# A hybrid layer on one core: the output projection's squares, norms and first feed-forward weights are rearranged, and the last attention chains change their queue

## The chip, the cores and the metric

The kernel runs on one core of one Trainium2 chip. The metric is the device time of one execution in microseconds (us), less is better. The core has TensorE (PE; its weight loads are listed as PEld), VectorE (DVE), ScalarE (ACT), GpSimd (POOL) and SyncE (SP). In this kernel SP issues nearly every DMA, in one order that is fixed when the program is built.

## The reference

One layer over 2,048 frames with 16 learned meta tokens in front (T = 2,064), width 1,024, in float32. What matters here is cut from it:

```python
p = rms_norm(h, norm_mix_pre) @ w_in                     # oa: RG-LRU, ob: attention, oc: RWKV-7, from slices of p
mixed = jnp.concatenate([oa, ob, oc], axis=-1) @ w_out   # the output projection
h = h + rms_norm(mixed, norm_mix_post)
f = causal_dwconv(rms_norm(h, norm_ffn_pre) @ ffn_up, ffn_conv)    # 2 x 2816 columns, 3 taps
gate, val = jnp.split(f, 2, axis=-1)
f = (jax.nn.gelu(gate, approximate=True) * val) @ ffn_down
h = h + rms_norm(f, norm_ffn_post)
```

Here `rms_norm(x, g) = x * rsqrt(mean(x * x) + 1e-6) * g`. The attention group has 8 heads of width 64, is causal, and its softmax is weighted by forget gates.

## The kernel before

Every large product is made of three float32r products: an operand is split into a high part (a copy by ACT, L1594 or L166) and a low part (the difference, by DVE or POOL, L1595 or L167), and `mm3` multiplies high by high (L172), high by low (L173) and low by high (L174). The program is written out in full in Python, and each engine's list of instructions is put in its final order when the program is built: a scheduler that works with estimated durations takes, for each engine, the instruction that comes first in the source among those that it holds ready. On the chip each engine then goes through its own list strictly in order, and waits at an instruction whose inputs are not there, whatever stands ready behind it. `tc.issue_after(ins)` keeps instructions behind `ins` in the list of its engine.

The stages that the change touches, in order of time:

- **End of the attention** (class `Attn`). For each head and each block of 512 queries, `weights` makes scores (L681, L682), exponentials on ACT (L686), the products with v (`po`, L704) and, on POOL and partly DVE, the sum of the exponentials (`acc`, L725). When a block's last group is through, `ending` puts three steps on a list that is worked off later: `total` (the sum over partitions by PE, L751 and L752, then the DMAs `scr_den<-acc`, L754, and `dcol<-scr_den`, L755), `invert` (reciprocal, then the DMAs L760 and L761) and `scale` (multiply, then the DMA L765 into `scr_mix`). Each of the five DMAs needs the one before it to have landed. `ending` of one block runs inside `weights` of the next block, after its first group of scores. The last two blocks of all are those of head 7: queries 1,040 to 1,551 and 1,552 to 2,063.
- **Output projection** (`w_out_tile`): 17 tiles of tokens in `FFN_TILES`, the first with 2 rows, the others with 128. A tile loads its slice of `scr_mix` (L165, one buffer `raw`), splits it into `mh` and `ml` (two buffers each), multiplies by the resident weights `woh`, `wol` (48 matmuls of 512 columns into two banks `pswo`), then `add_normed` squares both banks (ACT, L1513, with a sum), scales them (DVE, L1522), adds the residual `wx` (L1523), and `rstd_of` squares the result for the next norm (ACT, L116 or L118). ACT's squares have to be written somewhere: they go into `mh`. Tiles 0 to 6 fill gaps of PE during the attention; tiles 7 and 8 (`HELD`) stay behind the products of the last but one block; tiles 9 to 12 need that block's result, tiles 13 to 16 that of the last block.
- **Norms for the feed-forward** (`ffn_norm`): load a tile of `h` (`xt<-scr_h`, L1555, three buffers), scale it (DVE, L1556), transpose it (PE, L1561), copy it into the quarters `q`. For the first third of the tokens (7 tiles) one such norm follows each output tile from tile 8 (`LATE`) on; after the seventh, `ffn_sums` makes the combined quarters t1 to t4 on POOL (L1589).
- **Feed-forward, up** (`ffn_up`): 3 thirds of the tokens times 22 column blocks of 128 give 66 units. A unit makes four products of quarters by 7 (a Strassen-like scheme, `PRODUCTS`), each of 12 matmuls of 344 columns, in three banks. ACT copies the banks of p1, p5 and p6 into `ga`, `vb` and `u2` before another product is added to them. The weights of the next unit are loaded and split while a unit runs (`ahead.operand`). The 7 weights `ws` and 7 token operands `xs` of the very first unit are made ahead of it. Of their buffers, 4 of 10 for weights (`uw`) and 3 of 8 for tokens (`xo`) exist beside the output projection; the rest takes over its memory. For the second and third part of the tokens, `between` runs one norm at the start of each unit.

Of the kernel before, what the change touches and what calls it, by code (L numbers as in the profile page):

```python
# [18 lines left out]
P = 128  # L19
# [419 lines left out]
class Attn:  # L439
# [209 lines left out]
    def weights(self, h, b, keys, queries, fill):  # L649
# [80 lines left out]
        def ending(po, acc):  # L730
# [13 lines left out]
            rb = []  # L744

            def total():
# [7 lines left out]
                nc.sync.dma_start(scr["den"][h : h + 1, ts], acc[0:1, :n])  # L754
                nc.sync.dma_start(dcol[:, :g], scr["den"][h, ts].rearrange("(p c) -> p c", c=g))  # L755

            def invert():
                rb.append(self.t([64, 512], "rb"))
                nc.vector.reciprocal(dcol[:, :g], dcol[:, :g])
                nc.sync.dma_start(scr["rden"][h, ts].rearrange("(p c) -> p c", c=g), dcol[:, :g])  # L760
                nc.sync.dma_start(rb[0][:, :n], scr["rden"][h : h + 1, ts].broadcast_to([64, n]))  # L761

            def scale():
                nc.vector.tensor_tensor(o[:, :n], o[:, :n], rb[0][:, :n], op=ALU.mult)
                nc.sync.dma_start(scr["mix"][256 + 64 * h : 256 + 64 * h + 64, ts], o[:, :n])  # L765
# [36 lines left out]
    def run(self, pool):  # L802


        ready = []
# [17 lines left out]
        for step in ready:  # L823
            self.weights(*step, lambda share: None)
# [659 lines left out]
def w_out_tile(core, pool, psum, scr, w, x, meta, gain, s, rows, v):  # L1484
# [65 lines left out]
def ffn_norm(core, pool, psum, scr, s, rows, rs, gain, quarters, sup):  # L1550

    nc = core.nc
    xt = pool.tile([P, D], F32, tag="nt_x", name=core.n("xt"))
    t0 = s + META - HALO
    nc.sync.dma_start(xt[:rows], scr["h"][t0 : t0 + rows, :])  # L1555
# [140 lines left out]

POOLED = (3, 6), (6,)
# [10 lines left out]
def ffn_up(core, raws, ring, pool, banks, w_up, cw, scr, between, tokens):  # L1708
# [8 lines left out]
    ws = [ahead.operand(i) for i in range(7)]  # L1717
    xs = [tokens(0, i) for i in range(7)]
# [15 lines left out]
    for at, (sup, j) in enumerate(units):  # L1734
# [9 lines left out]
        for i, (name, (_, _, at_)) in enumerate(PRODUCTS.items()):  # L1744
# [7 lines left out]
            if j == NFF - 1 and more:  # L1752
                xs[i] = tokens(sup + 1, i)
            if more:
                ws_next.append(ahead.operand(i))
            if name == "p1":
                ga = s("ga")
                nc.scalar.activation(ga, ps, AF.Copy)
            elif name == "p5":
                vb = s("vb")  # L1760
                nc.scalar.activation(vb, ps, AF.Copy)
            elif name == "p6":
                u2 = s("u2")
                nc.scalar.activation(u2, ps, AF.Copy)
# [151 lines left out]
LATE = 8  # L1916
# [297 lines left out]
```

## Time and profile before

| | us |
|---|---|
| median of 3 timed runs | 3066.63 |
| lowest, highest | 3063.35, 3073.84 |
| profiled execution, its own time as the page gives it: the span from first to last instruction | 3071.8 |
| PE, DVE, ACT, POOL busy | 2921.6, 2054.8, 1482.3, 1358.8 |
| mean granted TensorE clock | 0.969 |

No time of the profiled execution outside its span is recorded. In the lists of the profile, L172 is line 172 of the kernel before; a bracket such as [6.86 <-ACT xo L1594] gives the time for which the engine stood idle just before the instruction and what ended it. SPq marks DMAs that SP issues; those are not counted as busy.

### The profile page before, as it was taken

The page shows a single profiled execution, that of the slowest core. Times are in us where ns is not written, and L with a number is a line of the kernel's source. Part 1 is how long each engine was busy: PE and PEld are TensorE (multiplying, and loading weights), DVE is VectorE, ACT ScalarE, POOL GpSimd, SP SyncE. Part 2 cuts the span into 40 slices and gives each one's busy share as a digit, 9 for nine tenths or more (in the row PEclk, how much of TensorE's full clock was granted, in tenths as well). Part 3 has the DMA queues.
Part 4 walks back from the last instruction along what each step waited for, and adds up shares of the span by engine and source line. Part 5 has one row for each costly group of instructions (what it writes and reads, how often), then busy time and mean ns, then how long its engine had stood idle before and what let it go on. Part 6 is the DMA issues. An engine that isn't in the chain of part 4 may idle for free. (4 is left out here: it accounts for less than half of the span.)

```text
span 3071.8 us, 52793 instructions
## 1 busy us (share of the span) xinstructions
PE 2921.6 (95%) x18694; PEld 2495.2 (81%) x18694; DVE 2054.8 (67%) x3934; ACT 1482.3 (48%) x2853; POOL 1358.8 (44%) x1589
## 2 busy tenths in 40 slices
PE   6999999999989999999989899999999999999998
PEld 6998898888876654665558899999999998787876
DVE  5268645656667785556635788888778786547766
ACT  4245332443336553555534656666566665324333
POOL 1001121122114555667842457445655444547765
PEclk9998999999988898999999999999999999999999
DMA  6776578466654346535245555566777765435444
GB/s 211 244 237 207 161 244 287 156 211 204 196 153 94 88 104 199 133 99 122 62 129 173 168 182 180 169 201 208 214 215 216 219 189 171 161 104 171 149 160 144
DMA packets 467818, 532.58 MB, mean 173 GB/s; under 512 B 85488, under 2 KB 355514, under 8 KB 466000
## 3 DMA queue, kind: packets, MB, share of 16 engines
q1 hardware_dynamic: 467168, 528.81, 56.5%
q8 instruction: 147, 2.41, 0.3%
q14 instruction: 119, 0.97, 0.1%
q0 software_dynamic: 384, 0.39, 0.0%
HBM read 369.11 MB, written 159.95 MB: 172 GB/s over the span
## 5 line engine op out<-in xcount | busy, mean ns | idle before, releaser
L172 PE MATMUL psu<-xo,uw 128*128 128x344 f32 x1848 | 589.9, 323 | 16.7 <-ACT xo L1594 6.9
L173 PE MATMUL psu<-xo,uw 128*128 128x344 f32 x1848 | 592.6, 321 | 0.0
L174 PE MATMUL psu<-xo,uw 128*128 128x344 f32 x1848 | 582.9, 320 | 0.0
L172 PE MATMUL psp<-xh,wh 128*128 128x384 f32 (+2 forms) x1152 | 383.6, 333 | 4.1 <-ACT wh L166 2.4
L174 PE MATMUL psp<-xh,wl 128*128 128x384 f32 (+2 forms) x1152 | 380.7, 331 | 3.5 <-DMA wl<-scr_wk 3.5
L173 PE MATMUL psp<-xl,wh 128*128 128x384 f32 (+2 forms) x1152 | 380.5, 330 | 0.0
L172 PEld LDWEIGHTS psu<-xo,uw 128*128 128x128 f32 x1848 | 346.9, 188 | 20.3 <-ACT xo L1594 7.1
L1595 DVE TENSOR_TENSOR uw<-uq,uw 128x512 fp32r<-128x512 f32 x341 | 316.2, 933 | 70.3 <-ACT uw L1594 63.7
L173 PEld LDWEIGHTS psu<-xo,uw 128*128 128x128 f32 x1848 | 347.9, 188 | 0.3 <-DVE xo L1595 0.3
L174 PEld LDWEIGHTS psu<-xo,uw 128*128 128x128 f32 x1848 | 346.5, 188 | 0.0
L1594 ACT ACTIVATE uw<-uq 128x512 fp32r<-128x512 f32 x462 | 287.9, 627 | 110.1 <-PE psu L174 48.7
L686 ACT ACTIVATE p<-sc,bias 128x512 f32<-128x512 f32 (+4 forms) x352 | 195.8, 590 | 178.5 <-PE sc L682 146.3
L1725 DVE SCALAR_TENSOR_TENSOR uy<-psu,ffn_cols,uy 128x342 f32<-128x342 f32 (+1 forms) x396 | 223.9, 567 | 60.7 <-ACT uy L1723 59.1
L559 DVE TENSOR_REDUCE mc<-mx 128x1 f32<-128x512 f32 (+6 forms) x352 | 190.3, 565 | 100.9 <-PE mx L554 75.8
L1731 POOL TENSOR_TENSOR uy<-uy,uy 128x342 f32<-128x342 f32 (+1 forms) x132 | 140.6, 1065 | 253.2 <-DVE uy L1725 77.4
L725 POOL TENSOR_TENSOR acc<-acc,p 128x512 f32<-128x512 f32 (+3 forms) x208 | 221.8, 1068 | 60.3 <-ACT p L686 23.9
L1595 POOL TENSOR_TENSOR uw<-uq,uw 128x512 fp32r<-128x512 f32 x121 | 177.9, 1470 | 125.0 <-ACT uw L1594 92.7
L174 PEld LDWEIGHTS psp<-xh,wl 128*128 128x128 f32 x1152 | 222.1, 193 | 13.0 <-issue 6.1
L172 PEld LDWEIGHTS psp<-xh,wh 128*128 128x128 f32 x1152 | 222.1, 193 | 10.7 <-issue 4.0
L173 PEld LDWEIGHTS psp<-xl,wh 128*128 128x128 f32 x1152 | 222.1, 193 | 7.6 <-issue 5.5
L1595 DVE TENSOR_TENSOR fo<-u,fo 128x896 fp32r<-128x896 f32 x88 | 112.6, 1279 | 121.3 <-ACT fo L1594 121.3
L1594 ACT ACTIVATE fo<-u 128x896 fp32r<-128x896 f32 x88 | 81.1, 922 | 206.3 <-POOL u L1841 106.8
(465 smaller groups left out, 6470.4 us busy)
## 6 DMA issues: line engine op xcount, KB each, us to landing
uq<-scr_us SPq DMA_DIRECT2D x220, 256.0 KB
uq<-in_ffn_up_dram SPq DMA_DIRECT2D x209, 256.0 KB
wl<-scr_wk SPq DMA_DIRECT2D x48, 512.0 KB
wh<-scr_wk SPq DMA_DIRECT2D x48, 512.0 KB
u<-scr_ff SPq DMA_DIRECT2D x88, 256.0 KB
scr_ff<-uy SPq DMA_DIRECT2D x110, 171.0 KB
raw<-in_w_in_dram SPq DMA_DIRECT2D x24, 512.0 KB
scr_wk<-wh SPq DMA_DIRECT2D x24, 512.0 KB
```

Of the source, the lines that this page charges most:

```text
L172: nc.tensor.matmul(out, ah, bh, start=first, stop=False, skip_group_check=more)
L173: nc.tensor.matmul(out, ah, bl, start=False, stop=False, skip_group_check=more)
L174: nc.tensor.matmul(out, al, bh, start=False, stop=last, skip_group_check=more)
L559: self.reduced = nc.vector.tensor_reduce(mc[:rows, i, ci : ci + 1], ps[:rows, : e - a], axis=AX.X, op=ALU.max)
L686: last = nc.scalar.activation(p[:rows, :w], ps[:rows, :w], AF.Exp, bias=bias[:rows, j : j + 1])
L725: eng.tensor_tensor(a, ps_[0][0][:rows, c0:n] if start and i == 1 else a, p[:rows, : n - c0], op=ALU.add)
L1594: core.nc.scalar.activation(hi, src, AF.Copy)
L1595: (eng or core.nc.vector).tensor_tensor(lo, src, hi, op=ALU.subtract)
L1725: stt(y[:, :n], src[:, i : n + i], cw[:, 44 * i + cc : 44 * i + cc + 1], y[:, :n], op0=ALU.mult, op1=ALU.add)
L1731: core.pooled = nc.gpsimd.tensor_tensor(v[:, :n], g[:, :n], v[:, :n], op=ALU.mult)
```

## The change

1. **Queue.** In the attention, the DMAs of `total`, `invert` and `scale` go through `self.queue`, which is SP and is set to GpSimd ahead of the last block's `weights`. `ending` reads it when it runs, so the chains of both blocks of head 7 are issued by GpSimd.
2. **Squares.** `w_out_tile` writes its squares into a bfloat16 tile `jk` of its own (2 KB a partition, one buffer) in place of `mh`.
3. **Norms.** Beside the output projection two norms (`NORMS`) follow each tile from tile 8 on, in place of one, so that the seventh comes at tile 11 in place of tile 14. The load of a norm's tile becomes a function of its own, `ffn_fetch`; in the feed-forward it is called one tile ahead of the norm that uses it.
4. **First unit.** Ahead of the first unit stand 3 weights and 4 token operands in turn, in place of 7 and 7. The other four weights and three token operands are made inside the first unit, one after each product, together with the next unit's weights; behind p1, p5 and p6 they stand behind the copy of that product's bank.

```diff
 ending():
-            rb = []
+            rb, queue = [], self.queue
 total(), invert(), scale():
-                nc.sync.dma_start(...)
+                queue.dma_start(...)
 Attn.run():
+        self.queue = self.nc.sync
 ...
-        for step in ready:
+        for i, step in enumerate(ready):
+            if i == len(ready) - 1:
+                self.queue = self.nc.gpsimd
             self.weights(*step, lambda share: None)

 w_out_tile():
-    junk = [mh[:, 4 * c : 4 * c + 4].rearrange("p k t -> p (k t)") for c in range(2)]
-    add_normed(core, pool, halves, rows, gain, xt, junk)
+    junk = pool.tile([P, D], BF16, tag="jk", name=core.n("jk"), bufs=1)
+    add_normed(core, pool, halves, rows, gain, xt, [junk[:, 512 * c : 512 * c + 512] for c in range(2)])
     nc.sync.dma_start(scr["h"][s : s + rows, :], xt[:rows])
-    return xt, rstd_of(core, v[:rows], xt[:rows], D, mh[:rows].rearrange("p k t -> p (k t)"))
+    return xt, rstd_of(core, v[:rows], xt[:rows], D, junk[:rows])

+def ffn_fetch(core, pool, scr, s, rows):
+    xt = pool.tile([P, D], F32, tag="nt_x", name=core.n("xt"))
+    t0 = s + META - HALO
+    core.nc.sync.dma_start(xt[:rows], scr["h"][t0 : t0 + rows, :])
+    return xt

 ffn_up():
-    ws = [ahead.operand(i) for i in range(7)]
-    xs = [tokens(0, i) for i in range(7)]
+    ws, xs, own = [], [], ahead
+    for i in range(UP_FIRST):                  # UP_FIRST = 3
+        xs.append(tokens(0, i))
+        ws.append(ahead.operand(i))
+    xs.append(tokens(0, UP_FIRST))
 ... in the loop over a unit's products, after mm3:
+            behind = nullcontext()
+            if name in ("p1", "p5", "p6"):
+                t = s({"p1": "ga", "p5": "vb", "p6": "u2"}[name])
+                copied = nc.scalar.activation(t, ps, AF.Copy)
+                ...
+                if at == 0:
+                    behind = core.tc.issue_after(copied.ins)
+            with behind:
+                if at == 0 and len(ws) < 7:
+                    ws.append(own.operand(len(ws)))
+                if at == 0 and len(xs) < 7:
+                    xs.append(tokens(0, len(xs)))
+                if j == NFF - 1 and more:
+                    xs[i] = tokens(sup + 1, i)
+                if more:
+                    ws_next.append(ahead.operand(i))

 output projection's loop:
-                if i >= LATE and todo:
-                    q, f, rows = todo.pop(0)
-                    ffn_norm(core, np_, ps_n, scr, f, rows, rs[q], g_fpre, quarters[0], 0)
+                for _ in range(NORMS if i >= LATE else 0):     # NORMS = 2
+                    if todo:
+                        q, f, rows = todo.pop(0)
+                        xt = ffn_fetch(core, np_, scr, f, rows)
+                        ffn_norm(core, ps_n, xt, f, rows, rs[q], g_fpre, quarters[0], 0)
 between():
-            elif todo:
-                q, f, rows = todo.pop(0)
-                ffn_norm(core, np_, ps_n, scr, f, rows, rs[q], g_fpre, quarters[sup], sup)
+            elif fetched:
+                q, f, rows, xt = fetched.pop(0)
+                fetch()
+                ffn_norm(core, ps_n, xt, f, rows, rs[q], g_fpre, quarters[sup], sup)
```

More of the change, by code (lines that the diff above doesn't have):

```diff
@@ L1695 @@
 EARLY = range(1, NFF, 2)
+UP_FIRST = 3
 POOLED = (3, 6), (6,)
@@ L1914 @@
 WIDE = (0, 5)
-LATE = 8
+LATE, NORMS = 8, 2
 HELD = 7, 8
@@ L2108, in hybrid_block_kernel, with fetch @@
         up = pool(p3, "up", 2, **early)
-        sums, ws, down = [iter(())], [], []
+        sums, ws, down, fetched = [iter(())], [], [], []
+        def fetch():
+            if todo:
+                q, f, rows = todo.pop(0)
+                fetched.append((q, f, rows, ffn_fetch(core, np_, scr, f, rows)))
         def between(sup, j):
```

38 lines of the change are left out of this document (14 added, 24 removed).

## The prediction

> **What bounds the kernel now.** I read the page first, then the busy time by stretches, then the waits of PE, and last the lists of single engines where PE loses time.
>
> ```profile
> PE 2921.6 (95%) x18694; PEld 2495.2 (81%) x18694; DVE 2054.8 (67%) x3934; ACT 1482.3 (48%) x2853; POOL 1358.8 (44%) x1589
> ...
> core 0: us, PE busy (x) PEld busy (x) DVE busy (x) ACT busy (x) POOL busy (x), PEclk, DMA share, GB/s
> 1560.00:1580.00 20.00, 14.02 (x52) 7.61 (x52) 6.83 (x17) 7.44 (x14) 13.17 (x24) 0.83 0.38 111
> 1600.00:1610.00 10.00, 5.33 (x18) 3.70 (x17) 9.26 (x13) 5.57 (x13) 5.17 (x4) 0.68 0.90 297
> 1690.00:1720.00 30.00, 20.90 (x116) 19.45 (x115) 25.07 (x33) 19.36 (x37) 12.62 (x8) 0.83 0.46 147
> 1780.00:1820.00 40.00, 35.16 (x224) 34.28 (x224) 33.36 (x50) 18.12 (x38) 17.32 (x13) 1.00 0.57 178
> 2050.00:2080.00 30.00, 27.93 (x178) 27.05 (x177) 23.74 (x37) 16.20 (x32) 14.89 (x11) 1.00 0.65 199
> 1820.00:1900.00 80.00, 80.00 (x508) 80.00 (x507) 70.46 (x104) 50.33 (x101) 59.69 (x46) 1.00 0.59 179
> 1701.97:1713.00 11.03, 11.03 (x57) 10.77 (x58) 11.03 (x9) 4.04 (x9) 7.66 (x5) 0.82 0.29 100
> ...
> 1607.79 0.43 PE pswo L172
> ...
> 1611.14 0.23 PE pswo L172
> ```
>
> PE is busy 95% of the span and the change takes no matmul away, so it can only win what PE loses to waiting, and that is little and in known places. The rows are stretches: length, then busy time by engine (PE first), then the granted clock. After an idle time the clock is low for a while: the last two rows, from the chain of waits, show one matmul of 512 columns every 0.43 us just behind a gap and every 0.23 us later. The places, with names:
>
> - **A**, the end of the attention (1560 to 1580): 20.00 − 14.02 = 6.0 us idle, and 11 matmuls at 0.43 in place of 0.23, 2.2 us. Together 8.2.
> - **B**, the third tile after it (1600 to 1610): 4.7 idle, and 8 slow matmuls, 1.6. Together 6.3.
> - **C**, from the output projection into the first units (1690 to 1720): 9.1 idle, and (1 − 0.82) × 11.03 = 2.0 for the clock. Together 11.1.
> - **D**, norms inside the feed-forward (1780 to 1820, 2050 to 2080): 4.8 + 2.1 = 6.9.
>
> All four make 32.5 us, 1.1% of the span: no gain beyond that is possible. About 0.3% (9.2 us) is what a measurement of this kernel can tell from no change.
>
> ```profile
> PE mx L751 <- ACT oh L748: 3.5, 1, 3.5
> PE pswo L172 <- ACT mh L166: 3.2, 2, 2.3
> PE pswo L174 <- DVE ml L167: 2.4, 1, 2.4
> ...
> PE psu L172 <- ACT xo L1594: 6.9, 1, 6.9
> ```
>
> These are PE's longest waits there: the last attention sum (A), the splits of output tiles (one of 0.9 us in A, 2.3 and 2.4 us in B), the split of a token operand (C).
>
> **The change, part by part.**
>
> *Queue (A).* SP's list, DVE's at the end, and a row of SP's waits:
>
> ```profile
> 1560.19 0.47 SPq L765 DMA_DIRECT2D scr_mix<-o  x1
> 1562.44 0.38 SPq L165 DMA_DIRECT2D raw<-scr_mix  x1
> ...
> 1575.33 0.28 SPq L754 DMA_DIRECT2D scr_den<-acc  x1
> ...
> 1586.41 0.46 SPq L765 DMA_DIRECT2D scr_mix<-o  x1
> 1586.92 0.58 SPq L1997 DMA_DIRECT2D g_fpre<-in_norm_ffn_pre_dram  x1
> ...
> 1591.97 1.27 DVE L1556 SCALAR_TENSOR_TENSOR xt<-xt,rsv,g_fpre 2x1024 f32<-2x1024 f32 x1 [5.59 <-DMA g_fpre<-in_norm_ffn_pre_dram]
> ...
> SPq L165 <- DMA scr_mix<-o: 1.8, 1, 1.8
> ```
>
> From 1575.33 to 1586.41 SP steps through the last block's chain, 11.1 us for five small DMAs, and everything behind it in SP's list (the gain g_fpre, the first norms, the first weights) waits; DVE then stands 5.6 us for g_fpre with the output tile's L1522 behind it. With the chain on POOL these loads go up to 11 us earlier, to soon after 1562–1575. What stays on SP is the load at 1562.44, which waits for head 7's first block (last row), now at the end of POOL's chain. The Trainium skill (DMA: Bandwidth & Descriptors, section "Issuing engines are not separate DMA queues") says that issuing from another engine saves only the issue time, since all DMAs share 16 engines. By it this part would be worth nothing on PE; the rows differ, since it is waits inside SP's list that delay others, not the transfers.
>
> What it costs stands on POOL. There the DMA instructions wait in line with the sums `acc`, and the PE products and the p buffers wait for those:
>
> ```profile
> 1552.84 2.64 POOL L725 TENSOR_TENSOR acc<-acc,p 128x512 f32<-128x512 f32 x2 [3.92 <-ACT p L686]
> 1560.91 1.27 POOL L725 TENSOR_TENSOR acc<-acc,p 128x512 f32<-128x512 f32 x1 [5.43 <-DVE rs L1517]
> ...
> L2023 POOL DMA_DIRECT2D scr_p<-zeros x12: 540/540/743, 1.3 to 10.7; - x12
> ...
> DMA to landing us min/median/max: 2.8/6.4/6.9
> ```
>
> The only DMAs that POOL issues now (L2023, at the start) took 0.54 us each on its list and 2.8 us to landing at best. Head 7's first chain holds POOL for 5 × 0.54 + 4 waits × 2.8 + about 1.0 for the reciprocal and the multiply = 14.9 us, and POOL has 3.92 + 5.43 = 9.35 us of idle there. So 5.6 us of sums could come late, at the best landing. PE's cover is output tile 8, whose 48 matmuls at 0.23 (11.0 us) need none of this, if they stand ahead of the late things in PE's list; in the trace they come behind them. Value for A: a gain of 3.0, since part of the 8.2 is the load order that goes and part the sum over partitions, which stays; bounds from a gain of 8.2 to a loss of 5.6 + 2.2 for the clock = 7.8, with slower landings in a rival.
>
> *Squares (B).* ACT's list:
>
> ```profile
> 1600.58 0.61 ACT L116 ACTIVATE mh<-wx 128x512 fp32r<-128x512 f32 x1
> ...
> 1601.93 1.04 ACT L166 ACTIVATE mh<-raw 128x1024 fp32r<-128x1024 f32 x1
> ```
>
> The split of tile 10 overwrites `mh` of tile 8, which is still the square's waste basket until 1601.1, so it starts at 1601.93, although its data were requested at 1575.8. With `jk` it can start when tile 8's matmuls are through. DVE's low part (the 2.4 us wait) follows, freed from the wait for g_fpre as well. Value 6.0 of 6.3, bounds 0 to 6.3. The squares cost the same (one writer, ACT, so one buffer adds no wait).
>
> *Memory.* `jk` adds 2,048 bytes to a pool whose lower end, by the tile sizes, has 960 bytes free above the tiles `mt` of the meta tokens' attention. So the pool now reaches 1,088 bytes into them and cannot be filled before they are done.
>
> ```profile
> 1190.49 0.62 SPq L640 DMA_DIRECT2D scr_mix<-mt  x1
> ...
> 1164.10 0.43 SPq L1480 DMA_DIRECT2D woh<-scr_wo  x1
> ...
> L173 PE MATMUL pswo<-wol,mh x108: 387/389/496, 1206.0 to 1403.3; 128*128 128x512 f32 x96, 128*2 128x512 f32 x12
> ```
>
> `woh` was loaded from 1164.1 on; `mt` ends after 1190.5, so tiles 0 to 6 start up to 26 us late. They end at 1403 now and tile 7 is held until about 1541, so 138 us of slack cover it; the work only moves to a stretch where PE is fuller. Value a loss of 2.0, bounds 0 and 6 (a quarter of those 26 us of filler).
>
> *Norms, two per tile.* Seven norms are moved, none added: transposes, copies and L1556 are the same. The sums of quarters start three tiles earlier:
>
> ```profile
> 1667.01 18.93 POOL L1589 TENSOR_TENSOR q<-q 128x344 f32<-128x344 f32 x16 [61.75 <-ACT q L56]
> ```
>
> 18.9 us of POOL that now end at 1686, just ahead of the first unit, end near 1651. POOL is idle 61.75 us before, so nothing is pushed. The second and third token operands are then ready early. Value inside C.
>
> *First unit (C).* ACT's list, then DVE's:
>
> ```profile
> 1694.79 1.65 ACT L1594 ACTIVATE uw<-uq 128x512 fp32r<-128x512 f32 x3
> 1696.35 5.05 ACT L1594 ACTIVATE xo<-q 128x1376 fp32r<-128x1376 f32 x4
> ...
> 1701.83 0.44 ACT L1758 ACTIVATE ga<-psu 128x344 f32<-128x344 f32 x1
> ...
> 1700.45 8.26 DVE L1595 TENSOR_TENSOR xo<-q,xo 128x1376 fp32r<-128x1376 f32 x4
> ```
>
> ACT makes three weights and four tokens before it copies p1's bank at 1701.83, and p6 cannot add to that bank before. After the change one token split (5.05 / 4 = 1.3) stands ahead of the copy and the other three (3.8), and the weights (1.65, and another 0.6), behind it: the copy can come about 6 us earlier. Next late is DVE: four low parts take 8.26, and the last four products last 4 × 12 × 0.157 (80.00 us / 508 matmuls) = 7.6 us on PE, so they run at DVE's pace with weights' low parts between. Hence 6.0 of 11.1; bounds 2 (the copy was not what held p3 to p4) to 9 (unit 1's products fill the rest).
>
> *Fetch one tile ahead (D).*
>
> ```profile
> DMA xt<-scr_h: 20.2, 7
> ...
> 1739.78 0.49 PE L1561 MATMUL pst<-ident,xt 128*128 128x128 f32 x3
> ...
> 1741.51 0.38 SPq L1555 DMA_DIRECT2D xt<-scr_h  x1
> ...
> 1747.96 1.28 DVE L1556 SCALAR_TENSOR_TENSOR xt<-xt,rsv,g_fpre 128x1024 f32<-128x1024 f32 x1 [3.33 <-DMA xt<-scr_h]
> ```
>
> DVE waits 20.2 us in 7 places for these loads. But a load is issued right behind the transposes that free a buffer (1739.78, 1741.51): the three buffers already keep it as early as they allow, and DVE's multiply stands at once behind it. The edit moves the load in the source, not the moment at which a buffer is free. Value 0, bounds 0 to 6.9.
>
> **Sum:** A 3.0 + B 6.0 + C 6.0 + D 0 − memory 2.0 = 13.0 us, so 3071.8 → 3058.8 on the profiled execution. Its span is 5.2 us above the median of the runs; on the median's scale 3066.6 − 13.0 = 3053.6, rounded 3054.
>
> **Rivals.**
>
> 1. *POOL's queue is slow (slower).* Place: head 7's chains. If POOL's DMAs land in the median 6.4 us of L2023 in place of 2.8, the first chain holds POOL for 2.7 + 25.6 + 1.0 = 29.3, less 9.35 idle = 20.0 us of late sums, and tiles 9 and 10 get their data as late, so B is not won; with 2.2 for the clock, 2.0 for memory and C's 6.0 won the result is +18.2, 3085. With a landing L the late sums are 2.7 + 4L + 1.0 − 9.35 = 4L − 5.65 and the whole is 4L − 5.65 + 2.2 + 2.0 − 6.0 = 4L − 7.45: slower by over 9.2 from L = 4.2 us on. For it: the median. Against: those 12 stood in line behind each other, these come singly. The Trainium skill (SBUF — State Buffer, section "SBUF: two separate sides") gives a mechanism for it: GpSimd writes the descriptors of its DMAs through a port that certain DVE instructions lock; a DMA of about 620 ns then took about 3100. No run here shows that. By 2.5 us more per landing, an estimate from that page, L would be 5.3 and the result +13.8. Chance 0.14.
> 2. *C only changes its name (no change).* DVE's 8.26 us start when the memory of the output projection is free, as before, PE waits for DVE in place of ACT, and A stays as it is: B 6.0 + C 2.0 − 2.0 = 6.0 won, 3061. For it: DVE is busy 11.03 of 11.03 us in 1701.97 to 1713. Against: unit 1 needs only weights. Chance 0.22.
> 3. *The fetch works (faster still).* If D goes as well: 19.9 won, 3047; with all of A and C, 3036. For it: the 20.2 us are DVE's largest wait there. Chance 0.10.
> 4. *The new order is worse elsewhere (slower).* The lists are rebuilt from estimates; one new gap of C's size (11.1) in the attention or the tiles 9 to 12, with B lost in it, and only C won: 11.1 + 2.0 + 2.2 − 6.0 = +9.3, 3076. Chance 0.08.
>
> **How the numbers follow.** Forecast 0.46 (3054, own range 3044 to 3057), rivals 0.14, 0.22, 0.10, 0.08. Faster by over 0.3%: 0.46 + 0.10 = 0.56; within: 0.22; slower: 0.14 + 0.08 = 0.22. The range runs from 3038 (nearly all of rival 3) to 3078 (rival 4 and the mild part of rival 1); the rest of rival 1 lies outside.
>
> **What would show it.** A: at 1575 SP issues loads in place of L754 to L765, and POOL's list holds ten DMAs. B: L166 starts within 2 us of the last matmul of the tile two before, and the stretch behind the third tile has PE at 10 of 10. C: L1758 follows the last output tile within 3 us, and the wait PE <- ACT xo is under 2 us. D: the wait DMA xt<-scr_h in the feed-forward is still about 20 us. POOL: its sums in the last block end within 6 us of 1570. The forecast is wrong if PE's idle time from 1540 to 1720 does not fall by at least 8 us.

## The result, and the profile after

The changed kernel takes 3063.64 us, the kernel before 3069.71 (medians of 22 runs each): a ratio of 0.9979, 95% interval 0.9971 to 0.9987, or 6.4 us less. The forecast was 13.0 us less. The direction was right and the forecast twice the truth. This section shows where the gain was made and where part of it went.

The page and the stretches after, in the columns of those before. The stretch 1540 to 1720 is given for both kernels. The changed kernel ends its last output product 7.3 us earlier (1682.17, before 1689.46), so 1690 to 1720 does not hold the same work in both; 1682 to 1712 is the place that corresponds to it.

```profile
PE 2910.2 (95%) x18694; PEld 2487.6 (81%) x18694; DVE 2057.7 (67%) x3934; ACT 1479.1 (48%) x2853; POOL 1365.7 (45%) x1599
...
core 0: us, PE busy (x) PEld busy (x) DVE busy (x) ACT busy (x) POOL busy (x), PEclk, DMA share, GB/s
1540.00:1720.00 180.00, 168.06 (x816) 135.88 (x815) 107.02 (x164) 85.76 (x184) 72.37 (x73) 0.98 0.49 160
1560.00:1580.00 20.00, 13.96 (x58) 7.85 (x57) 8.64 (x17) 7.67 (x15) 12.91 (x25) 0.83 0.34 95
1600.00:1610.00 10.00, 10.00 (x55) 8.17 (x54) 10.00 (x13) 5.85 (x15) 5.18 (x3) 1.00 0.92 270
1682.00:1712.00 30.00, 25.98 (x160) 24.48 (x159) 25.56 (x30) 19.39 (x37) 12.35 (x7) 1.00 0.40 127
1690.00:1720.00 30.00, 27.36 (x165) 25.58 (x164) 29.18 (x37) 21.46 (x39) 16.31 (x10) 1.00 0.51 159
```

Before:

```profile
1540.00:1720.00 180.00, 160.25 (x738) 127.63 (x738) 95.54 (x152) 79.39 (x171) 60.44 (x59) 0.93 0.48 153
```

Place A (1560 to 1580) is as it was: PE 13.96 us busy, 14.02 before, the clock at 0.83 in both. B (1600 to 1610) is closed, with PE busy all 10 us and the clock back at 1.00. C (1690 to 1720) has gone from 9.1 us of idle PE to 2.6, or to 4.0 in the stretch that corresponds. From 1540 to 1720 PE's idle time fell from 19.75 to 11.94, by 7.8 us. The forecast called itself wrong below 8.

The lists and waits behind that. First ACT's two splits of the tiles 10 and 11 (output tiles counted from 0) and the copy of p1's bank; then PE's longest wait from 1530 to 1625 and, in the last rows, three of PE's waits in the whole span:

```profile
1593.28 1.06 ACT L166 ACTIVATE mh<-raw 128x1024 fp32r<-128x1024 f32 x1 [4.46 <-PE pswo L173]
1603.48 1.05 ACT L166 ACTIVATE mh<-raw 128x1024 fp32r<-128x1024 f32 x1
...
1688.72 0.43 ACT L1768 ACTIVATE ga<-psu 128x344 f32<-128x344 f32 x1
...
PE mx L751 <- ACT oh L748: 4.7, 1, 4.7
...
PE psu L172 <- DVE vb L1787: 6.9, 5, 4.4
PE psu L172 <- ACT vb L1768: 3.1, 2, 1.8
PE psu L172 <- ACT ga L1768: 2.4, 1, 2.4
```

Before, PE's waits for DVE's `vb` in the whole span:

```profile
PE psu L172 <- DVE vb L1769: 3.8, 5, 1.3
```

The split of tile 10 starts at 1593.28, where it started at 1601.93 before. The wait for the last attention sum stays (4.7, was 3.5); the waits for splits of output tiles and the 6.9 us for `xo` are gone. But one wait of 4.4 us for `vb` is new (the longest was 1.3), and it does not lie in the stretch on which the prediction worked. It lies 50 us further on:

```profile
1740.00:1750.00 10.00, 5.78 (x39) 5.47 (x38) 7.25 (x11) 2.18 (x4) 2.90 (x2) 0.94 0.54 173
1750.00:1760.00 10.00, 9.86 (x47) 9.86 (x48) 8.24 (x13) 6.05 (x13) 5.78 (x5) 0.72 0.59 194
```

Before, the same clock times:

```profile
1740.00:1750.00 10.00, 10.00 (x67) 10.00 (x66) 6.67 (x11) 6.81 (x14) 1.45 (x2) 1.00 0.66 218
1750.00:1760.00 10.00, 10.00 (x68) 9.98 (x67) 8.68 (x17) 6.05 (x12) 4.93 (x3) 1.00 0.73 222
```

PE idles 4.2 us in 1740 to 1750, and over the ten microseconds behind that its clock is 0.72: 67 + 68 products became 39 + 47. That is where C's gain went.

To compare kernels whose work lies at shifted times, the program behind the attention is cut at the same products of PE: **a** from product 600 with v to the last product of output tile 11 (products and tiles counted from 0; 48 products a tile), **b** to the last output product, **c** the first three units of the feed-forward (252 products), **d** the next six (504), **e** the rest. One profiled execution each, in us:

| kernel | ratio to before, 95% | a | b | c | d | e |
|---|---|---|---|---|---|---|
| before | | 127.2 | 58.8 | 53.4 | 88.8 | 1240.5 |
| changed | 0.9979 (0.9971 to 0.9987) | 121.1 | 57.2 | 48.7 | 94.9 | 1236.3 |
| changed, again | 0.9977 (0.9963 to 0.9991) | 121.7 | 57.1 | 48.7 | 95.0 | 1239.6 |

The change won 5.8 in a, 1.7 in b, 4.7 in c, and gave 6.2 back in d (means, with e6 below, whose lists are the same): 6.0 in all, against 6.4 of the whole kernel. e is no evidence either way: it differs by over 3 us between executions of the changed kernel itself.

### The profile page after: what moved, and what is told of

Read it like the earlier page. It is cut to its first block, busy times and chain, and to the rows that moved or that the text cites. A ratio compares the mean times of both kernels' runs of the same rounds, so it can differ in the third digit from the quotient of the medians.

```text
span 3061.7 us, 52809 instructions
## 1 busy us (share of the span) xinstructions
PE 2910.2 (95%) x18694; PEld 2487.6 (81%) x18694; DVE 2057.7 (67%) x3934; ACT 1479.1 (48%) x2853; POOL 1365.7 (45%) x1599
## 3 DMA queue, kind: packets, MB, share of 16 engines
q1 hardware_dynamic: 466716, 528.27, 56.5%
## 4 chain that ended last, share of the span: by engine, by line
PE 34%; DVE 5%; DMA 5%; POOL 3%; issue 3%; ACT 1%; SPq 0%; POOLq 0%; DVEq 0%; ACTq 0%
PE psu L172 8%; PE psu L173 8%; PE psu L174 8%; PE psd L172 2%; PE psd L173 2%; PE psd L174 2%; DMA u<-scr_ff 2%; DMA xt<-scr_h 1%; DVE uw L1603 1%; PE pswo L172 1%; PE pswo L174 1%; PE pswo L173 1%; DVE fo L1603 1%; DVE uy L1738 1%; POOL u L1858 1%
## 5 line engine op out<-in xcount | busy, mean ns | idle before, releaser
L725 POOL TENSOR_TENSOR acc<-acc,p 128x512 f32<-128x512 f32 (+3 forms) x208 | 221.7, 1068 | 53.1 <-DVE acc L725 23.9
```

The lines of the kernel that those rows point to most:

```text
L725: eng.tensor_tensor(a, ps_[0][0][:rows, c0:n] if start and i == 1 else a, p[:rows, : n - c0], op=ALU.add)
```

## The experiments

### One part undone at a time

`e6_nofetch` puts the load back right ahead of its norm; `e2_nojk` puts the squares back into `mh`; `e4_syncq` sends the chains through SP; `e3_up7` puts back the old order ahead of and inside the first unit; `f4_norms1` has one norm a tile. The fence has lines cut from these edits; the remarks behind # are not in the code.

```diff
e6 -fetched.append((q, f, rows, ffn_fetch(core, np_, scr, f, rows)))   +fetched.append((q, f, rows))
e6 +xt = ffn_fetch(core, np_, scr, f, rows)        # right ahead of ffn_norm
e2 +junk = [mh[:, 4 * c : 4 * c + 4].rearrange("p k t -> p (k t)") for c in range(2)]
e4 -self.queue = self.nc.gpsimd                    +self.queue = self.nc.sync
e3 +ws = [ahead.operand(i) for i in range(7)]      +xs = [tokens(0, i) for i in range(7)]
f4 -LATE, NORMS = 8, 2                             +LATE, NORMS = 8, 1
```

> The changed kernel with each token tile's load written right ahead of its norm again. The lists of all five engines come out instruction for instruction as in the changed kernel, so every theory expects the changed kernel's time, 0.998 of the kernel before; it is a second look at the changed kernel, and tells how far one execution's stretches scatter: the stretch from the fourth to the tenth unit near 95 us again if the 6 us given back there are no accident, near 89 to 91 if they are.

> The changed kernel with the squares written over mh again, as in the kernel before; the queue, the norms and the first unit stay changed. Theory (the buffer for squares carries stretch B): tile 10's split waits for the squares again, PE loses about 6 us behind the third tile after the attention, and the memory price of 5 us goes at the same time: within 2 us of the changed kernel, 0.997 to 0.999 of the kernel before. Rival (the loads that the other queue lets forward carry B): B stays closed and the memory price is won back, 5 us faster than the changed kernel, 0.996.

> The changed kernel with the chains of head 7 on SP's queue again. Theory (the other queue wins about 2 us at the end of the attention, and stretch B belongs to the buffer for squares): 1 to 3 us slower than the changed kernel; SP steps through the chain from about 1575 to 1586 and the gain g_fpre is loaded behind it. Rival 1 (GpSimd's small DMAs are slow, and the queue costs more than it brings): 1 to 4 us faster. Rival 2 (the queue also carries B): 6 to 9 us slower.

> The changed kernel with the feed-forward's weights and tokens in the order of the kernel before (all seven weights and seven tokens first, splits ahead of the bank copies). Theory (the split order wins 4.7 us up to the fourth unit and loses 7 us at 1740 to 1756, where DVE stands 6.2 us for a token tile and the next bank waits for it): the wait PE <- ACT xo of about 7 us comes back, the gap at 1740 goes, the kernel is 0 to 3 us faster than the changed one. Rival 1 (the gap at 1740 has to do with the load alone and not with the split order): the gap stays and the 4.7 us are lost, 4 to 5 us slower than the changed kernel. Rival 2 (C only changed its name): the same time within 1 us.

> The changed kernel with one norm behind each late output tile in place of two. Theory (two norms per tile only take 8 transposes out of each of the last tiles, 1.0 to 1.7 us, and put them into the first): within 2 us of the changed kernel, 0.9975 to 0.9985 of the kernel before. Rival (the norms moved forward make stretch B and the first tiles behind the attention tighter, as the kernel without the buffer for squares hints, 2.7 us won there in place of 5.3): 2 to 3 us faster, 0.997.

| kernel | ratio to before, 95% | a | b | c | d | e |
|---|---|---|---|---|---|---|
| e6 | 0.9991 (0.9973 to 1.0009) | 121.3 | 57.1 | 48.8 | 95.1 | 1236.0 |
| e2 | 0.9990 (0.9974 to 1.0005) | 124.5 | 58.6 | 48.5 | 95.0 | 1239.9 |
| e4 | 0.9962 (0.9947 to 0.9976) | 119.0 | 56.3 | 49.7 | 90.4 | 1238.3 |
| e3 | 0.9999 (0.9984 to 1.0013) | 121.3 | 57.1 | 53.6 | 89.9 | 1240.7 |
| f4 | 0.9991 (0.9978 to 1.0003) | 121.1 | 58.0 | 48.7 | 97.4 | 1236.5 |

- **Fetch:** in e6 all five engines have the same lists as in the changed kernel, instruction for instruction, and the stretches agree within 0.3 us. The fetch edit is no edit. Its ratio, as much as it differs, measures the spread of such comparisons.
- **Squares:** e2 loses 3.1 in a and 1.5 in b. That is `jk`'s worth where two norms and the queue are present, but not by way of B: tiles 10 and 11 take 26.1 in e2, as in the changed kernel. 2.6 of the 3.1 are lost by the end of tile 9, where e2's second chain on GpSimd takes 20.4 us and the changed kernel's 15.9.
- **Queue:** the kernel is faster with the chains on SP, against the theory put down for it. This was run again on another chip (below).
- **First unit:** e3 loses the 4.9 in c and gets 5.1 back in d. By c and d together (143.5 against 143.6) splitting the weights wins nothing. The times put its worth at about 6 us with an interval of some 5 either way; the stretches show 3 us of that at most, in e, where executions of the changed kernel itself differ by as much.
- **Norms:** f4 loses 0.9 in b and 2.4 in d.

### The queue by itself, and again

`f6_queue` is the kernel before with the queue edit alone; `h7_syncq_again` is e4 on another chip.

> The kernel before, with the chains of head 7 on GpSimd's queue and nothing else changed: term A of the prediction by itself. The prediction's view: 3 us faster (0.999), and part of stretch B with it, since the gain g_fpre no longer stands behind the chain on SP. Theory now (GpSimd's DMAs hold the chain longer, 15 us from the first to the last in place of 11, and the list that is planned with it sets the last sum's product ahead of the tile's products): 0 to 4 us slower, 1.000 to 1.0013.

> The changed kernel with the chains of head 7 on SP once more, as e4_syncq, on another chip. Theory (the GpSimd queue costs 4 to 6 us of what the change brings): 0.9955 to 0.997 of the kernel before, and tile 9 again 92 us behind the 600th product with v. Rival (the first trial was lucky): 0.998, as the changed kernel.

| kernel | ratio to before, 95% | a | b | c | d | e |
|---|---|---|---|---|---|---|
| f6 | 0.9986 (0.9971 to 1.0001) | 121.9 | 58.8 | 53.0 | 92.0 | 1240.0 |
| h7 | 0.9962 (0.9946 to 0.9978) | 121.1 | 56.5 | 49.7 | 90.3 | 1239.8 |

Alone, the queue wins 5.3 in a, by the stretches; for the whole kernel the interval just passes 1. In company it wins nothing there. Where it wins is seen in SP's list and ACT's split of tile 10 in f6:

```profile
1576.55 0.53 SPq L2000 DMA_DIRECT2D g_fpre<-in_norm_ffn_pre_dram  x1
...
1598.12 1.06 ACT L166 ACTIVATE mh<-raw 128x1024 fp32r<-128x1024 f32 x1
```

The gain `g_fpre` goes out at 1576.55, ten microseconds earlier than before, DVE is through with the tile sooner, and the split stands at 1598.12 in place of 1601.93. All of the gain lies there: tiles 10 and 11 take 24.1 us in f6 and 30.8 before, while the part of a up to the end of tile 9 gets longer (97.8, was 96.4). With `jk` and the chains on SP the two tiles take 27.0 and 27.1 (e4, h7). So the queue and `jk` close the same gap, B, by two ways. With both, the gap is closed once, and of the queue only the costs are left. They are seen in GpSimd's list in the changed kernel (brackets: idle time before the instruction, and what ended it), and in DVE's (last row):

```profile
1552.63 0.58 POOL L754 DMA_DIRECT2D scr_den<-acc  x1 [2.75 <-ACT acc L753]
...
1564.00 0.54 POOL L765 DMA_DIRECT2D scr_mix<-o  x1 [0.84 <-DVE rs L87]
...
1570.60 0.48 POOL L725 TENSOR_TENSOR acc<-acc,p 128x144 f32<-128x144 f32 x1
...
1582.10 0.56 POOL L754 DMA_DIRECT2D scr_den<-acc  x1 [2.22 <-ACT acc L753]
1587.72 0.49 POOL L755 DMA_DIRECT2D dcol<-scr_den  x1 [5.06 <-DMA scr_den<-acc]
1591.82 0.48 POOL L760 DMA_DIRECT2D scr_rden<-dcol  x1 [3.61 <-DVE dcol L759]
1593.66 0.54 POOL L761 DMA_DIRECT2D rb<-scr_rden  x1 [1.36 <-DMA scr_rden<-dcol]
1597.42 0.55 POOL L765 DMA_DIRECT2D scr_mix<-o  x1 [3.22 <-DVE o L764]
...
1591.17 0.34 DVE L759 RECIPROCAL dcol<-dcol 16x32 f32<-16x32 f32 x1 [13.71 <-DMA dcol<-scr_den]
```

and in SP's list, first in the changed kernel and then in e4:

```profile
1578.94 0.38 SPq L2015 DMA_DIRECT2D g_fpre<-in_norm_ffn_pre_dram  x1
```
```profile
1574.26 0.23 SPq L754 DMA_DIRECT2D scr_den<-acc  x1
...
1582.04 0.46 SPq L765 DMA_DIRECT2D scr_mix<-o  x1
```

The last block's chain takes 15.9 us on GpSimd, from 1582.10 to its end, and 8.2 on SP in e4 (11.5 in the kernel before). Counted from product 600 with v (1503.5 in the changed kernel, 1497.6 in e4) it ends 94.5 us behind it on GpSimd and 84.9 on SP. If the part of a up to the end of tile 9 is taken alone, the changed kernel needs 95.0, 96.0 and 96.3 in three executions, the six kernels with the chains on SP beside `jk` 92.0 to 94.1, the kernel before 96.4.

The loads that the queue lets go earlier and the chain get in each other's way, as far as four traces tell. The late link (5.06 us) stands just behind the loads that SP sends from 1578.94 on. While it lasted, the DMA engines moved 295 GB/s, and DVE did nothing at all; during the first chain they moved 12. Two more executions of these lists have the late link at the same place (4.5 and 4.6 us, 214 and 242 GB/s), f6 has it at the third transfer (6.3 us, 335 GB/s), and in all of them DVE is idle meanwhile. No run moved the loads alone.

### The memory of the squares

`f3_mem` is the kernel before with an unused tile of the size of `jk` in the same pool; `e1_jkpool` gives `jk` a pool of its own below, so that `woh` comes early again; `f1_jk7` does so too and uses `jk` only from tile 7 on.

```diff
e1 -junk = pool.tile([P, D], BF16, tag="jk", ...)   +junk = core.jk.tile(...)    # core.jk = pool(p2, "jkp", 1, **right)
f1 +if own: whole = core.jk.tile(...)               # own: i >= 7
f1 +else:   whole = mh.rearrange("p k t -> p (k t)")
f3 +pool.tile([P, D], BF16, tag="jk", name=core.n("jk"), bufs=1)     # never used, kernel before
```

> The kernel before, with a 2,048-byte tile declared in the output projection's pool and not used: the pool reaches over the meta tokens' tiles as in the changed kernel, and nothing else is changed. Theory M (it is the late load of woh that costs inside the attention): tiles 0 to 6 end 35 us later, 4 to 5 us slower, 1.0015. Theory J (it is the use of the buffer in tiles 0 to 6, which lets their splits start earlier and so reorders the lists, as the pool of its own with 12 us lost ahead of 1503 us hints): the tiles end later and the time is the same, 1.000.

> The changed kernel with the 2,048 bytes for the squares in a pool of their own below the output projection's pool, so that only these bytes and no longer woh lie over the meta tokens' attention tiles. Theory (the memory price is real and larger than the 2.0 us that I gave it): tiles 0 to 6 of the output projection end at about 1415 us again and not at 1449, the stretch from the last recurrence product to the last attention product gets 4 to 6 us shorter, and the kernel is about 5 us faster than the changed one (0.9962 of the kernel before). Rival (the slack of 138 us covers the delay): the tiles come early again, the time stays within 2 us of the changed kernel (0.998).

> The changed kernel, but the buffer for squares is used from output tile 7 on only and lies in a pool of its own, so that tiles 0 to 6 (inside the attention) run as in the kernel before, load of woh and order of instructions included. Theory (the changed kernel wins about 10 us behind 1503 us and gives about 4 back inside the attention, because the buffer delays or reorders tiles 0 to 6): the 4 us come back, 0.9965 of the kernel before. Rival (the attention's part is only the scatter between executions): as fast as the changed kernel, 0.998.

| kernel | ratio to before, 95% | a | b | c | d | e |
|---|---|---|---|---|---|---|
| f3 | 0.9994 (0.9978 to 1.0009) | 127.3 | 58.8 | 53.1 | 89.6 | 1238.0 |
| e1 | 1.0013 (0.9998 to 1.0028) | 121.5 | 57.1 | 50.9 | 89.8 | 1241.5 |
| f1 | 0.9976 (0.9960 to 0.9991) | 121.2 | 57.1 | 48.1 | 98.1 | 1241.2 |

f3 shows no cost of the overlap by itself (at most 3 us, by its interval): the slack of 138 us can cover it. e1 was to be faster than the changed kernel and is no faster than the one before, although its stretches behind the attention are as good. Its edit differs from that of f1, which is 0.0037 or 11 us faster, only in that `jk` is used in the tiles 0 to 6 too. The profiled executions do not show where the 11 us are: e1 comes to product 600 with v at 1501.9 and f1 at 1501.1. PE's waits for the keys of the attention from 1130 to 1540, in e1, in f1, in the kernel before and in the changed one:

```profile
PE mx L554 <- DMA k<-scr_cl: 9.2, 6, 2.9
```
```profile
PE mx L554 <- DMA k<-scr_cl: 2.9, 2, 2.1
```
```profile
PE mx L554 <- DMA k<-scr_cl: 1.1, 2, 0.8
```
```profile
PE mx L554 <- DMA k<-scr_cl: 4.7, 2, 3.0
```

In e1 the lists of the attention come out in another order from about 1,214 us on, and loads of keys come later: 6.3 us more of that wait than in f1. Whether that makes the 11 us is open. So is the changed kernel's own share. Twelve of the kernels have its lists up to product 600 with v and come there at 1497.6 to 1512.4 us; six have those of the kernel before and come there at 1497.8 to 1510.4. Both means are 1503.1, with some 4 us of uncertainty in their difference: no cost is seen, and one of 2 us could not be.

### Where C's gain went

The chain that ended last in 1736 to 1752, by line, in the changed kernel, and its first piece; then rows of SP's and DVE's lists there; and, in the last fence, the chain in the kernel before:

```profile
by line: DMA xt<-scr_h 80.7%; DVE uw L1603 17.5%; DVE xt L1564 8.0%; DVE uy L1738 6.6%; issue 3.1%; DVE psu L1790 2.7%; DVE psu L1784 2.6%; SPq L1678 2.3%; DVEq L1603 0.4%; SPq L1557 0.1%
...
1735.55 7.17 DMA xt<-scr_h
```
```profile
1734.63 0.82 SPq L1678 DMA_DIRECT2D uq<-scr_us  x2
1735.55 0.37 SPq L1557 DMA_DIRECT2D xt<-scr_h  x1
...
1742.75 1.28 DVE L1564 SCALAR_TENSOR_TENSOR xt<-xt,rsv,g_fpre 128x1024 f32<-128x1024 f32 x1 [6.17 <-DMA xt<-scr_h]
```
```profile
by line: PE psu L174 26.6%; PE psu L172 26.6%; PE psu L173 25.8%; POOL uy L1731 11.6%; issue 9.5%; PE pst L1561 5.5%; ACT uw L1594 4.0%
```

Before, PE's own products end last there. After, it is one load of a token tile and the norm on DVE behind it, with `vb` behind that. Where no edit aims at it, the load is issued 52 to 54 us behind the last output product, in the changed kernel as before: it stands in SP's list behind loads of weights, and those wait for DVE and GpSimd, not for PE. Its buffer was free 51.4 us behind the last output product before and is free 46.7 us behind it now: before, the load went out at once, and now SP's list keeps it. With C's edit PE, DVE and the buffer get there 4.7 us earlier, and DVE finds nothing: it waits 6.17 us where it waited 3.33 before, and now PE runs out of other work before DVE's sum is through. All twenty profiled kernels, by DVE's wait for that token tile (e5, f5: the second one, since the first comes early), PE's wait for `vb` behind it (in unit 4, counted from 0; in e2 in unit 3) and d:

| kernels | first-unit edit | DVE's wait | PE's wait | d |
|---|---|---|---|---|
| before, e3, f3, f6 | no | 3.3 to 4.4 | none | 88.8 to 92.0 |
| e1, e4, h6, h7, i1 | yes | 4.0 to 5.6 | 0 to 1.7 | 88.9 to 92.2 |
| h1 | yes | 5.0 | 3.4 | 90.8 |
| changed (twice), e6, e2, e5, f1, f2, f4, f5, h5 | yes | 5.5 to 6.6 | 3.5 to 4.6 | 93.3 to 100.1 |

Up to about 5 us of DVE's wait PE hardly notices; above, PE waits too in all but one kernel (h7, 5.6), and d is longer by 4.5 us and more (2.0 in h1, of which below). The wait comes with the first-unit edit: e3 takes the edit back, and wait and loss go. But the edit does not always bring it. Five kernels have the edit and keep its gain, with c and d together at 138.6 to 141.0 (before 142.2, changed 143.6).

Three ways around the wait were tried: a fourth buffer with the load two tiles ahead (`e5_xt4`), the norm held behind the copy of p6's bank (`h5_hold`), both also with the chains on SP (`f5_jk7_sync_xt4`, with `jk` as in f1; `h6_sync_hold`), and the loads on GpSimd's queue (`h1_xtpool`). `f2_jk7_sync` is f1 with the chains on SP. Lines cut from the edits:

```diff
e5 +nps = [pool(p3, "np1", 1, **early), np_, np_, np_]      +fetch()        # a second one at j == 1
h5 +if name == "p6" and norm:
h5 +    with core.tc.issue_after(copied.ins):
h5 +        norm()                                          # returned by between()
h1 -core.nc.sync.dma_start(xt[:rows], ...)                  +core.nc.gpsimd.dma_start(xt[:rows], ...)     # feed-forward only
```

> The changed kernel with a fourth buffer for the token tiles in the feed-forward and the fetch two tiles ahead. Theory (the split order's gain of 4.7 us is given back between the fourth and the tenth unit because DVE stands 5.5 to 6.6 us for a token tile whose load waits for one of three buffers): the load of the first late tile is issued before the first unit, DVE's waits for xt fall from 20 us to under 8, the stretch from the fourth to the tenth unit gets 5 to 6 us shorter (94.9 to about 89), and the kernel is 4 to 6 us faster than the changed one, 0.996 of the kernel before. Rival (DVE's wait is only where it shows, and PE waits for DVE's work as such): DVE's wait goes, PE's wait for vb stays, same time.

> The changed kernel with each norm inside the feed-forward written behind its unit's third bank copy (p6) in place of ahead of the unit, so that in DVE's list it stands behind a bank's sum that it stood ahead of; the load stays on SP. Theory (what costs is not the load but that the bank's sums stand behind the waiting norm in DVE's list): DVE's waits for xt fall from 20 us to under 8, PE's wait for vb at 1740 goes, stretch from the fourth to the tenth unit 89 to 91, 4 to 5 us faster than the changed kernel. Rival (another instruction of DVE's takes the place): stretch 93 or more.

> The changed kernel with the feed-forward's token tiles loaded on GpSimd's queue in place of SP's. Theory (the load of the first late tile is ready to go at 1728.5 us, when the transposes free its buffer, and stands 7 us in SP's list behind weights that wait for DVE and GpSimd; so DVE, which has the norm next, stands 6 us and the bank's sum behind it): the load goes out 4 to 7 us earlier, DVE's wait at 1740 falls under 3 us, the stretch from the fourth to the tenth unit falls from 95 to 90 us, 4 to 5 us faster than the changed kernel. Rival (the transfer is slow because the DMA engines are full at that time, whichever queue it is on): DVE waits 5 us or more, stretch 94 to 96.

> As f1_jk7, and the chains of head 7 on SP's queue. Theory (the GpSimd queue costs 3 to 4 us at the end of the attention, and the early use of the buffer costs 4): 14 to 15 us faster than the kernel before, 0.9952; tile 8 ends about 81 us behind the 600th product with v, where it takes 84 in the changed kernel. Rival (the 9 us that the first trial of SP's queue won were an accident of its chip and runs): 0.9965, as f1_jk7.

> The version that the runs so far point to: squares in a buffer of their own from tile 7 on, chains on SP, two norms per tile, the split order, and four token buffers with the fetch two tiles ahead. Theory: the 10 us of f2_jk7_sync and the 4 to 5 us that the fourth buffer keeps: 14 to 15 us faster than the kernel before, 0.9953. Rival (gains do not add, the next wait in DVE's list takes their place): 0.997, as f2_jk7_sync.

> h5_hold with the chains of head 7 on SP: the best parts of all runs so far. Theory: 12 us faster than the kernel before from the chains on SP, and the stretch from the fourth to the tenth unit at 88 to 91 us, where that run had 90.4 already: 0.995 to 0.9965.

| kernel | ratio to before, 95% | a | b | c | d | e |
|---|---|---|---|---|---|---|
| e5 | 0.9981 (0.9968 to 0.9994) | 120.9 | 57.1 | 49.4 | 100.1 | 1234.8 |
| h5 | 0.9981 (0.9965 to 0.9996) | 121.8 | 57.1 | 47.8 | 95.4 | 1240.9 |
| h1 | 0.9955 (0.9938 to 0.9972) | 121.4 | 57.1 | 49.1 | 90.8 | 1235.2 |
| f2 | 0.9970 (0.9955 to 0.9986) | 120.2 | 56.3 | 49.3 | 93.3 | 1239.9 |
| f5 | 0.9990 (0.9974 to 1.0007) | 121.4 | 56.3 | 52.7 | 96.3 | 1238.9 |
| h6 | 0.9962 (0.9948 to 0.9975) | 120.5 | 56.8 | 48.8 | 92.2 | 1240.3 |

e5 and h5 miss, and f5 misses both of its expectations, with 6.46 us of DVE's wait; f2 is as slow as its rival, and h6 lies within its range. With the fourth buffer the first norm goes to 1703.04, and the wait comes back with the next one:

```profile
1703.04 2.30 DVE L1564 SCALAR_TENSOR_TENSOR xt<-xt,rsv,g_fpre 128x1024 f32<-128x1024 f32 x1
...
1741.96 1.29 DVE L1564 SCALAR_TENSOR_TENSOR xt<-xt,rsv,g_fpre 128x1024 f32<-128x1024 f32 x1 [6.11 <-DMA xt<-scr_h]
```

In h5 the norm's wait is 6.13 us, and nothing is won. In h1 the load does not go earlier either, on GpSimd's list:

```profile
1735.67 0.58 POOL L1557 DMA_DIRECT2D xt<-scr_h  x1
```
```profile
1742.83 1.28 DVE L1564 SCALAR_TENSOR_TENSOR xt<-xt,rsv,g_fpre 128x1024 f32<-128x1024 f32 x1 [5.04 <-DMA xt<-scr_h]
...
1755.23 1.28 DVE L1564 SCALAR_TENSOR_TENSOR xt<-xt,rsv,g_fpre 128x1024 f32<-128x1024 f32 x1 [0.83 <-DMA xt<-scr_h]
```

but DVE's wait is 1.1 us shorter, and the later ones shrink. DVE's waits for token tiles in the feed-forward, in the changed kernel and in h1:

```profile
DVE xt L1564 <- DMA xt<-scr_h: 20.5, 7, 6.2
```
```profile
DVE xt L1564 <- DMA xt<-scr_h: 14.2, 6, 5.0
```

PE's waits for DVE's `vb` from 1690 to 1840 in h1:

```profile
PE psu L172 <- DVE vb L1787: 3.9, 2, 3.4
```

The long one is still there (3.4, was 4.4); what has gone is the 3.1 us of waits for ACT's `vb` in the units 6 and 7. d falls to 90.8, as expected and not in the expected way, so that hit was luck. h1 is 14 us faster than the kernel before, and its interval just touches that of the changed kernel, so its lead over that is likely and not certain. No run, then, has removed the wait by sending the load earlier.

### The two best edits together, and the changed kernel against itself

`i1_sync_xtpool` is e4 with h1's edit; `i2_after_again` is the changed kernel, unedited, on that chip.

> The changed kernel with the chains of head 7 on SP and the feed-forward's token tiles on GpSimd's queue: the two queues the other way round than in the changed kernel. Theory (the chains on SP bring 5 us against the changed kernel, the token loads on GpSimd's queue bring 5 to 6 between the seventh and the 37th unit, in different places): 15 to 18 us faster than the kernel before, 0.994 to 0.995. Rival (both gains are the same 5 us, which any re-planning of the lists behind 1570 us brings): 0.996, as each alone.

> The changed kernel itself once more, beside the version with both queues the other way round. Expected: 0.998 of the kernel before (0.9971 to 0.9987 as first measured); stretches 121 us from the 600th product with v to tile 11, 49 for the first three units, 95 for the next six. A rival would be 0.9957, the forecast itself, if the first measurement fell on a bad chip.

i1: 0.9954 (0.9937 to 0.9970), with a to e 121.7, 58.6, 49.7, 88.9, 1234.6. i2 stands in the first table. e4's gain over the changed kernel is 5 us, h1's about 7, that of both together nearly 8. That looks like two edits which take the same thing again, but i1's interval holds the sum of the two gains as well. They do not save in d at the same waits: with the chains on SP PE's wait in unit 4 is only 1.0 and 1.7 us (e4, h7) and later ones of up to 1.9 remain; in h1 the wait in unit 4 remains and the later ones are short. The swap of the queue alone wins 2 us in f2 over f1, 6 in h6 over h5 and nothing in i1 over h1.

## Why the prediction was right in sign and twice too large

Two steps of its sum failed. A was credited with 3.0 us, and the queue wins nothing beside `jk`. C's 6.0 were carried to the end of the kernel, and 6.2 us were lost again behind it.

- **A, forecast −3.0, measured −0.6** (96.4 to a mean of 95.8 up to the end of tile 9), and those 0.6 are not the queue's: there the queue costs 1.4 us alone (f6, 97.8) and 1 to 4 beside `jk` (92.0 to 94.1 with the chains on SP). The list of SP changed as predicted: at 1578.94 `g_fpre` goes out and GpSimd holds ten DMAs. The price of the first chain on GpSimd was smaller than feared: it took 11.9 us (forecast 14.9 from the row L2023), and GpSimd's sums ended at 1571, within the bound of 6 us. What failed is the credit. The 5.6 us of DVE's wait for `g_fpre` end at 1591.97, behind A's stretch; they are part of what holds up tile 10, which is B, and B was already counted as won by `jk`. One gap was entered under two edits; f6 shows the queue winning it alone.
- **B, forecast −6.0, measured −5.2** (30.8 to a mean of 25.6 for the tiles 10 and 11). The size was right, and the mechanism named works: with `jk` and without the queue the two tiles take 27. But the queue alone does it too (f6 24.1, e2 26.1). The split of tile 10 starts 5.2 us behind the last product of tile 8 (1588.03) and not within 2.
- **Stretch b, not forecast, −1.7.** Two norms a tile take transposes out of the last output tiles, and f4, with one, has 58.0: about half of it. e2, without `jk`, has 58.6.
- **Memory, forecast +2.0, not seen.** Late filler tiles cost nothing that f3 shows, and the changed kernel's executions come to product 600 as early as those with the lists of the kernel before. The scatter would hide 2 us.
- **C, forecast −6.0, measured −4.7 in c, and +6.2 in d.** In its place C came out well: the wait for `xo` is gone, though the copy of p1's bank stands 6.5 us behind the last output product and not 3. The step that failed is the step from there to the end. C's value was carried to the end of the span without asking which in-order wait comes next and whether it moves with it. The row was in the prediction itself, under D: 3.33 us of DVE's wait at 1747.96, with a value of 0. It cost PE nothing as long as PE came no earlier; in the changed kernel, with PE 4.7 us earlier, it is 6.17 and PE waits too.
- **D, forecast 0 with bounds 0 to 6.9 of gain.** The edit does nothing, as forecast, and DVE's waits are 20.5 us where they were 20.2. But the bounds left out a loss at that place, and that is where C's gain was lost.
- **Rivals.** Rival 2 (6.0 won) has the measured size and A right (it stayed as it was), but not C: C won 4.7 in its place and not 2.0, and the loss came 50 us later, behind a load. Rival 1, a slow queue, is right in sign, since GpSimd's queue costs 5 us against SP's in e4 and h7 (0 to 6 in the other pairs), but far smaller than its 20 us of late sums. By the Trainium skill (DMA: Bandwidth & Descriptors, "Issuing engines are not separate DMA queues") issuing from another engine saves only the issue time. By that the queue would be worth nothing on PE; in f6, with the queue alone, stretch a is 5.3 us shorter, because what moved was the waiting in SP's list. By the Trainium skill (SBUF — State Buffer, "SBUF: two separate sides") certain DVE instructions lock the port through which GpSimd writes descriptors, and a DMA of about 620 ns then took about 3100. That is not what happened here: each of GpSimd's DMAs stood 0.48 to 0.58 us on its list, the first chain was through in 11.9 us, and during the late link of the second (5.06 us) DVE was idle.

## What to carry to other kernels

Before a gain in one stretch is carried to the end of the kernel, look for the next instruction whose time the edit does not move (here a load in SP's list, 53 us behind the last output product) and work out how much earlier its users may come: beyond that slack the gain may be lost again, as it was here and in most of the kernels with this edit. List for every gap all the edits that would close it, and credit it once; of the others only their costs remain. An edit that leaves every engine's list as it is can be seen without a run to be worth nothing.

## What the runs showed of the hardware

Behind an idle time of PE of 4.2 us the granted clock was 0.72 over the next ten microseconds, so the gap cost the 4.2 us and nearly 3 more ((1 − 0.72) × 10 = 2.8). A chain of five small DMAs, each waiting for the one before, took 11.9 us on GpSimd's queue while the DMA engines moved 12 to 15 GB/s, and 13.8 to 20.3 us where a link fell among loads at 214 to 335 GB/s; DVE was idle during each of those links. And the stretches a, b, c and d repeat within some 0.6 us in three executions of equal lists, while the 1,500 us ahead of them scatter by 14.8 among twelve kernels: in a program like this a late edit of a few microseconds is read from the stretches of a trace, an early one only from many runs.
